# Eight instead of five feed-forward groups of a layer in seven-product form, three pairs of them adjacent; input sums on GpSimd; the kernel's beginning in another order

## The chip, the cores and the metric

The kernel runs on one core of a Trainium2 chip. Its engines are TensorE (PE; PEld is its weight load), VectorE (DVE), ScalarE (ACT), GpSimd (POOL) and SyncE (SP, which here only issues transfers). The metric is the device time of one execution in microseconds (us), the median of several runs.

## The reference

Two layers of a decoder trunk over 512 tokens of width 1024. Each layer mixes tokens by three parallel branches and then runs a gated feed-forward part with a causal convolution of three taps:

```python
D_MODEL = 1024; SEQ = 512; DEPTH = 2; D_FF = 3 * D_MODEL
for l in range(DEPTH):
    h = rms_norm(x, norm_mix[l])
    ...  # three branches, gated and merged
    x = x + merged @ w_out[l]
    h = rms_norm(x, norm_ffn[l])
    ff_g, ff_u = jnp.split(h @ ffn_up[l], 2, axis=-1)
    ff_g = causal_dwconv(ff_g, ffn_conv_w[l], ffn_conv_b[l])
    x = x + (jax.nn.gelu(ff_g) * ff_u) @ ffn_down[l]
return rms_norm(x, norm_final)
```

All is float32. The change concerns `h @ ffn_up[l]` and the first norm.

## The kernel before

**Precision by splitting.** Every float32 matrix is split into a rounded high part and the remaining low part; a product is three matmuls (low by high, high by low, high by high). `split_to` (line 149) does it for weights: ACT copies a 128x1024 block `raw` to `wh` (L169), DVE subtracts it to get `wl` (L170). `hl_split` does the same for activations (L182, L183). A block of 128x1024 weights is called a unit. The pool `wp` holds three pairs `wh`, `wl`, so the split of a unit waits until the matmuls of the third unit before it are done; its subtraction must end before the unit's own matmuls begin.

**The feed-forward part.** The normed activations lie transposed in `xh`, `xl` (128 rows x 8 blocks x 512 tokens). The 24 blocks of hidden channels come in three chunks of eight (HC = 8). A block needs a gate product and an up product, each one unit and 24 matmuls of 512 columns (`f_group`, L222 and L228); two blocks are a group of four units. After the products `hidden` runs the convolution (ACT L398, DVE L402 twice), the gelu (ACT L945), the product with the up half (DVE L950) and a split (L182, L183). After each chunk `t_section` (L265) multiplies by `ffn_down` and DVE adds the result to the residual (L918). This happens for two halves of the output.

**Seven-product form.** For the groups in `QUADS` the 2x2 block product (two halves of the contraction, gate and up as the other dimension; two halves of the tokens) is done with seven instead of eight block products. `x_sums` (line 930) makes sums of token halves once a layer with eight DVE instructions on 128x1024 (L934, L937) in the buffers S8 and S10 and splits the four that are multiplied into S1, S2, S3, S7. `quads` (line 953) then runs seven units of 24 matmuls of 256 columns (`q_mm`, L255). Its weights arrive as four blocks `quad`, two in S8 and two in S10, and are combined in place by four DVE additions (L168) before the splits. The seven weights have the letters a to g: a, f and d are blocks as they came (0, 2 and 3), b, c, e and g are sums. DVE also combines the seven results: L969, L970, L973, L979, L982. The products accumulate in PSUM banks t (a and d), s (b and f), s (c and g) and o (e).

**Order.** The tile framework makes an in-order list for each engine from the program and priorities; each engine then runs its list strictly in order and waits on semaphores. `plan` (line 113) is the order of the units' transfers and splits; in a group in `QUADS` it reads a b c d e, then the first unit of the next group, f g. `quads` runs that `f_group` between e and f. All weight transfers are on SP's queue, and the SP waits at the first one whose buffer is not free. S8 and S10 exist once, so the blocks of one seven-product group can be fetched only when the last splits that read the previous ones are done. `dma_to` and `split_to` run ahead of the use by two and three units.

**The beginning.** SP fetches the first block of x, the norm's gain row, weights and the remaining x; ACT and DVE norm a token block (`Norm.rows`), PE transposes its eight 128x128 blocks (`Norm.turn`, L350) and ACT and DVE split them. 18 matmuls on zeros (L110) stand ahead. `t_section` for the section `mv` starts as soon as the first token block is there; its first two units need only the contraction blocks 0 to 3.

## Time and profile before

| quantity | value |
|---|---|
| median of 3 runs (lowest, highest) | 1932.69 us (1932.33, 1933.23) |
| the profiled execution's own time | 1932.97 us |
| its span | 1931.2 us |
| PE busy | 1907.6 us (99%) |
| DVE busy | 1241.8 us (64%) |
| ACT busy | 825.3 us (43%) |
| POOL busy | 88.4 us (5%) |
| granted TensorE clock, mean | 0.996 |

The busy share of PE is the union of pipelined matmuls, so 99% says that hardly a moment passes without one in flight; how fast they follow each other is read from the starts in the timeline. The "chain that ended last" on the page follows the work back from the last instruction. A timeline row gives start, duration, engine, source line, operation, output and inputs, shape, number of merged instructions and, in brackets, idle time of the engine before it and what ended that. DVE's instructions overlap a little at their ends, so the step from one start to the next is shorter than a duration.

### The profile page before, as it was taken

How to read it: one execution, taken by the hardware profiler on the slowest of the kernel's cores; microseconds unless marked ns; L12 is line 12 of the kernel's file. 1: busy time of each engine (PE TensorE's matmuls, PEld its weight loads, DVE VectorE, ACT ScalarE, POOL GpSimd, SP SyncE). 2: the span in 40 equal slices, each digit the busy share in tenths (PEclk: the TensorE clock that was granted, in tenths of full speed). 3: DMA queues.
4: the chain of work that ended last, by engine and by line, in shares of the span. 5: the costliest groups of instructions: out<-in, count | busy, mean ns of one | idle time of the engine just before them, and what ended most of it. 6: DMA issues, size and time to landing. Idle time of an engine off the chain costs nothing.

```text
span 1931.2 us, 24656 instructions
## 1 busy us (share of the span) xinstructions
PE 1907.6 (99%) x9654; PEld 1591.0 (82%) x9654; DVE 1241.8 (64%) x2069; ACT 825.3 (43%) x1264; POOL 88.4 (5%) x154
## 2 busy tenths in 40 slices
PE   8999999999999999999999999999999999999997
PEld 6778888888788888888887888888877888888985
DVE  6897869644458557557558987794334765574763
ACT  5664444443335424334357444445323443352442
POOL 0012110000000000000000121000000000000000
PEclk9999999999999999999999999999999999999999
DMA  5248642322332323322332586223223243232222
GB/s 177 93 129 252 180 115 77 101 97 82 99 107 99 121 68 129 109 97 68 114 122 88 179 241 164 93 66 126 72 93 110 76 142 109 96 101 77 88 88 77
DMA packets 59349, 218.27 MB, mean 113 GB/s; under 512 B 7384, under 2 KB 7896, under 8 KB 57184
## 3 DMA queue, kind: packets, MB, share of 16 engines
q1 hardware_dynamic: 47088, 169.37, 26.9%
q0 software_dynamic: 10560, 43.54, 7.7%
q10 hardware_dynamic: 1584, 3.78, 0.6%
q8 instruction: 76, 1.25, 0.3%
q14 instruction: 41, 0.34, 0.1%
HBM read 196.72 MB, written 19.42 MB: 112 GB/s over the span
## 4 chain that ended last, share of the span: by engine, by line
PE 92%; DVE 3%; ACT 2%; issue 1%; DMA 1%; SPq 0%; POOLq 0%; ACTq 0%
PE A L222 34%; PE A L265 22%; PE A L228 17%; PE s L255 6%; PE t L255 3%; PE o L743 2%; PE o L255 1%; DVE wl L170 1%; PE o L669 1%; PE s L704 1%; PE t L756 1%; DVE m L402 1%; PE s L350 1%; ACT wh L169 1%; PE s L769 1%
## 5 line engine op out<-in xcount | busy, mean ns | idle before, releaser
L170 DVE TENSOR_TENSOR wl<-raw,wh 128x1024 fp32r<-128x1024 f32 x262 | 319.8, 1222 | 358.5 <-ACT wh L169 354.3
L222 PE MATMUL A<-xh,wl 128*128 128x512 f32 (+1 forms) x1392 | 545.5, 394 | 2.2 <-DVE m L402 0.7
L222 PE MATMUL A<-xl,wh 128*128 128x512 f32 (+1 forms) x1392 | 543.5, 392 | 0.0
L169 ACT ACTIVATE wh<-raw 128x1024 fp32r<-128x1024 f32 x262 | 276.6, 1057 | 334.0 <-PE A L265 141.7
L228 PE MATMUL A<-xh,wh 128*128 128x512 f32 (+1 forms) x1392 | 358.1, 393 | 0.0
L222 PEld LDWEIGHTS A<-xh,wl 128*128 128x128 f32 x1392 | 261.3, 188 | 63.4 <-DVE wl L170 3.5
L222 PEld LDWEIGHTS A<-xl,wh 128*128 128x128 f32 x1392 | 261.6, 188 | 59.5 <-issue 2.2
L228 PEld LDWEIGHTS A<-xh,wh 128*128 128x128 f32 x1392 | 255.5, 188 | 58.1 <-issue 1.2
L265 PE MATMUL A<-wh,S 128*128 128x512 f32 x832 | 261.8, 395 | 0.0
L265 PEld LDWEIGHTS A<-wh,S 128*128 128x128 f32 x832 | 155.9, 187 | 37.7
L265 PE MATMUL A<-wl,S 128*128 128x512 f32 x416 | 164.2, 395 | 0.0
L170 DVE TENSOR_TENSOR wl<-quad,wh 128x1024 fp32r<-128x1024 f32 x70 | 85.6, 1223 | 59.7 <-ACT wh L169 59.7
L169 ACT ACTIVATE wh<-quad 128x1024 fp32r<-128x1024 f32 x70 | 74.0, 1057 | 83.1 <-PE A L265 37.9
L402 DVE SCALAR_TENSOR_TENSOR m<-A,ch,m 128x511 f32<-128x511 f32 (+2 forms) x128 | 93.8, 743 | 10.1 <-ACT m L398 8.9
L265 PEld LDWEIGHTS A<-wl,S 128*128 128x128 f32 x416 | 78.0, 187 | 18.9
L255 PE MATMUL s<-S,wh 128*128 128x256 f32 x480 | 85.7, 281 | 0.0
L222 PE MATMUL A<-S,wl 128*128 128x512 f32 x192 | 75.9, 397 | 0.9 <-ACT S L594 0.9
L222 PE MATMUL A<-S,wh 128*128 128x512 f32 x192 | 75.2, 393 | 0.0
L255 PEld LDWEIGHTS s<-S,wh 128*128 128x128 f32 x480 | 74.0, 190 | 0.0
L846 ACT ACTIVATE th<-A 128x512 f32<-128x512 f32 x48 | 28.5, 595 | 104.7 <-PE A L228 78.1
L265 PE MATMUL A<-wx,S 128*128 128x512 f32 x288 | 69.3, 394 | 0.0
L758 ACT ACTIVATE g<-t 128x512 f32<-128x512 f32 (+2 forms) x48 | 25.1, 522 | 100.2 <-PE t L756 100.2
(264 smaller groups left out, 2802.6 us busy)
## 6 DMA issues: line engine op xcount, KB each, us to landing
raw<-in_wts_dram SPq DMA_DIRECT2D x274, 512.0 KB, 3.5
quad<-in_wts_dram SPq DMA_DIRECT2D x40, 512.0 KB, 4.4
S<-dh POOLq DMA_DIRECT2D x16, 512.0 KB, 6.9
S<-dl POOLq DMA_DIRECT2D x16, 512.0 KB, 7.8
dh<-th POOLq DMA_DIRECT2D x24, 256.0 KB, 4.3
dl<-m POOLq DMA_DIRECT2D x24, 256.0 KB, 3.6
S<-in_x_dram SPq DMA_DIRECT2D x4, 512.0 KB, 7.4
g<-gd POOLq DMA_DIRECT2D x8, 256.0 KB, 4.6
```

Of the source, the lines that this page charges most:

```text
L169: A.activation(out=h, in_=r, func=AF.Copy)
L170: V.tensor_tensor(out=l, in0=r, in1=h.bitcast(F32), op=ALU.subtract)
L222: T.matmul(ps, lhsT=a[:, k, :], rhs=b[:, k, :], start=(i == 0), stop=False)
L228: T.matmul(ps, lhsT=wh[:, k, :], rhs=b_h[:, k, :], start=False, stop=(i == n))
L255: T.matmul(ps[:, j * 256:(j + 1) * 256], lhsT=a[:, k, j * P:(j + 1) * P], rhs=x[b][:, k, :], start=start and j == 1 and i == 1, stop=j == ...
L265: T.matmul(ps, lhsT=a[k0 + j][:, tt], rhs=b[:, j, :], start=(start and i == 1), stop=(stop and i == n))
L350: ins = T.transpose(ps[:, c * P:(c + 1) * P], xn[:, k * P:(k + 1) * P], ident)
L402: V.scalar_tensor_tensor(out=acc[:, d:], in0=ps[:, :S - d], scalar=ch[:, cw + j * step:cw + j * step + 1], in1=acc[:, d:], op0=ALU.mult, o ...
L669: T.matmul(po[:, 0:129], lhsT=SD[:, sb * P:(sb + 1) * P], rhs=e.mv[:, sb, h, :], start=(sb == 0), stop=(sb == tb))
L743: T.matmul(po[:, h * 64:(h + 1) * 64], lhsT=pc[:, c * P:(c + 1) * P], rhs=e.av[:, c, h * 64:(h + 1) * 64], start=(c == 0), stop=(c == t))
L758: A.activation(out=pT[:, :n * P], in_=pp[:, :n * P], func=AF.Copy)
L846: A.activation(out=th, in_=pg, func=AF.Tanh, scale=0.5)
```

## The change

- `QUADS` has eight groups of a layer instead of five: (0,4), (0,6), (1,0), (1,2), (1,6), (2,0), (2,2), (2,6). Three pairs of a layer follow each other directly: (0,4) and (0,6), (1,0) and (1,2), (2,0) and (2,2).
- The order of the weights in such a group is a b c e d f g, with no unit of another group in between; `quads` runs a, b, c, e, d, then f and g, and no `f_group`.
- `x_sums` makes its eight sums on POOL.
- The beginning: the gain row comes on ACT's queue, the norm of the first layer is done by `squares` and `scaled`, the transposes of a token block are made in two halves, the instructions are tied in an order by `after`, and 24 instead of 18 matmuls on zeros stand ahead. Small transfers (`chan`, `rgw`, constants) come later.

```diff
@@ -37,7 +37,7 @@
 NK = 385
 
 
-QUADS = {(0, 4), (1, 0), (1, 4), (2, 0), (2, 4)}
+QUADS = {(0, 4), (0, 6), (1, 0), (1, 2), (1, 6), (2, 0), (2, 2), (2, 6)}
 SECTIONS = ("mv", "sm", "rx", "qk", "qi", "q", "k", "av", "mo")
 
 
...
@@ -106,7 +106,7 @@
     A.activation(out=warm, in_=half[:, 0:1], func=AF.Square)
     wz = S1("S9", (P, 512), BF)
     V.memset(wz, 0.0)
-    for _ in range(18):
+    for _ in range(24):
         T.matmul(accS(), lhsT=wz[:, 0:P], rhs=wz, start=True, stop=True)
 
     per = wts.shape[0] // depth
...
@@ -119,9 +119,8 @@
         for c in range(NH // HC):
             for g in range(HC // 2):
                 if (c, 2 * g) in QUADS:
-                    nxt = [(u + 4 + i, None) for i in range(4)]
-                    plan += [(u, o) for o in "abcde"] + nxt[:1] + [(u, o) for o in "fg"] + nxt[1:]
-                elif (c, 2 * g - 2) not in QUADS:
+                    plan += [(u, o) for o in "abcedfg"]
+                else:
                     plan += [(u + i, None) for i in range(4)]
                 u += 4
             plan += [(u + i, None) for i in range(HC)]
...
@@ -309,10 +310,37 @@
...
+        def squares(self, t):
+            lo, hi = slice(0, 512), slice(512, D)
+            with tc.high_priority():
+                xn = slot.tile([P, D], F32, tag=self.tags[t % len(self.tags)], name="xn")
+                ss = sml.tile([P, 2], F32, tag="ss", name="ss")
+                rs = sml.tile([P, 1], F32, tag="rs", name="rs")
+                if t < 2:
+                    V.tensor_tensor_reduce(out=xn[:, lo], in0=X(t, lo), in1=X(t, lo), scale=1.0, scalar=0.0,
+                                           op0=ALU.mult, op1=ALU.add, accum_out=ss[:, 0:1])
+                else:
+                    A.activation(out=xn[:, lo], in_=X(t, lo), func=AF.Square, accum_out=ss[:, 0:1])
+                A.activation(out=xn[:, hi], in_=X(t, hi), func=AF.Square, accum_out=ss[:, 1:2])
+                V.tensor_tensor(out=rs, in0=ss[:, 0:1], in1=ss[:, 1:2], op=ALU.add)
+                V.tensor_scalar(out=rs, in0=rs, scalar1=1.0 / D, scalar2=EPS, op0=ALU.mult, op1=ALU.add)
+                G.tensor_tensor(out=rs, in0=rs, in1=half[:, 0:1], op=ALU.pow)
+            self.xs[t], self.rs[t] = xn, rs
+
+        def scaled(self, t):
+            xn = self.xs.pop(t)
+            with tc.high_priority():
+                for cs in (slice(0, 512), slice(512, D)):
+                    v = V.scalar_tensor_tensor(out=xn[:, cs], in0=X(t, cs), scalar=self.rs[t], in1=self.g[:, cs],
+                                               op0=ALU.mult, op1=ALU.mult)
+            self.xn[t] = xn
+            return v
 
         def rows(self, t, sink=None):
             with tc.high_priority():
...
@@ -437,20 +461,45 @@
     for l in range(depth):
         if l == 0:
             res["src"] = x
+            nrm = Norm(norm_mix[0:1, :], ("S1", "S2", "S4", "S5"))
             nc.scalar.dma_start(out=ident, in_=const[:, K_ID:K_ID + P])
-            nrm = Norm(norm_mix[0:1, :], ("S1", "S2"), True)
-            nc.scalar.dma_start(out=kst[:, K_ID + P:], in_=const[:, K_ID + P:])
-            for t in range(1, NT):
-                dma_to(t)
+            dma_to(1)
+            nc.sync.dma_start(out=X(1), in_=x[P:2 * P, :])
+            dma_to(2)
+            for t in range(2, NT):
                 nc.sync.dma_start(out=X(t), in_=x[t * P:(t + 1) * P, :])
-            nrm.rows(0)
-            nrm.turn(0)()
-            split_to(1)
-            for t in range(1, NT):
-                nrm.rows(t)
-            mv_post = {t - 1: nrm.turn(t) for t in range(1, NT)}
-        ch = two.tile([P, NCH], F32, tag="ch", name="ch")
-        nc.scalar.dma_start(out=ch, in_=chan[l])
+            nrm.squares(0)
+            v = nrm.scaled(0)
+            with after(v):
+                split_to(1)
+            with after(st["pair"][0]), after(st["pair"][1]):
+                nrm.turn(0, (0,))()
+            with after(nrm.last[0]), after(nrm.last[1]):
+                nrm.squares(1)
+                split_to(2)
+            with after(st["pair"][0]), after(st["pair"][1]):
+                v = nrm.scaled(1)
+                ch0 = two.tile([P, NCH], F32, tag="ch", name="ch")
+                nc.scalar.dma_start(out=ch0, in_=chan[0])
+                nc.scalar.dma_start(out=kst[:, K_ID + P:], in_=const[:, K_ID + P:])
+                nrm.squares(2)
+                with after(v):
+                    nrm.turn(1, (0,))()
+                a1 = nrm.last
+                with after(a1[1]):
+                    v = nrm.scaled(2)
+                    nrm.turn(0, (1,))()
+                    nrm.turn(1, (1,))()
+                    nrm.squares(3)
+                    v = nrm.scaled(3)
+            mv_post = {0: nrm.turn(2), 1: nrm.turn(3)}
+        if l == 0:
+            ch = ch0
+        else:
+            ch = two.tile([P, NCH], F32, tag="ch", name="ch")
+            with after(a1[0]):
+                nc.scalar.dma_start(out=ch, in_=chan[l])
+        first = v
         e = SimpleNamespace()
         F_ = slice(96, 100)
         R_ = slice(64, 68)
...
@@ -931,10 +984,10 @@
             qa, qb = [S1(g, (P, 2, 4, 256)) for g in ("S8", "S10")]
             a = [qa[:, 0], qa[:, 1], qb[:, 0], qb[:, 1]]
             for n in (2, 3, 0, 1):
-                V.tensor_tensor(out=a[n], in0=xq[n][0].bitcast(F32), in1=xq[n][1].bitcast(F32), op=ALU.add)
+                G.tensor_tensor(out=a[n], in0=xq[n][0].bitcast(F32), in1=xq[n][1].bitcast(F32), op=ALU.add)
             for key, g, d, i0, i1, op in (("b", "S1", 3, 2, 3, ALU.subtract), ("c", "S2", 2, 0, 2, ALU.subtract),
                                           ("e", "S3", 0, 3, 0, ALU.subtract), ("f", "S7", 1, 1, 0, ALU.add)):
-                V.tensor_tensor(out=a[d], in0=a[i0], in1=a[i1], op=op)
+                G.tensor_tensor(out=a[d], in0=a[i0], in1=a[i1], op=op)
                 o = S1(g, (P, 2, 4, 256), dt=FR)
                 hl_split(a[d], o[:, 0], o[:, 1])
                 xq[key] = (o[:, 0], o[:, 1])
...
@@ -961,9 +1014,6 @@
                 A.activation(out=p1, in_=pa, func=AF.Copy)
             q_mm(pc, xq["b"])
             q_mm(pd, xq["c"])
-            q_mm(pa, xq[1], start=False)
-            with tc.high_priority():
-                A.activation(out=gt[:, :, 0:256], in_=three(pa), func=AF.Copy)
             q_mm(pb, xq["e"])
             with tc.high_priority():
                 V.tensor_tensor(out=u2, in0=p1, in1=pb, op=ALU.add)
...
@@ -971,7 +1021,9 @@
                 for j in range(2):
                     cs = slice(j * 256, (j + 1) * 256)
                     V.tensor_tensor(out=up[j][:, 256:512], in0=pc[:, cs], in1=tm[:, cs], op=ALU.subtract)
-            pg = f_group()
+            q_mm(pa, xq[1], start=False)
+            with tc.high_priority():
+                A.activation(out=gt[:, :, 0:256], in_=three(pa), func=AF.Copy)
             q_mm(pc, xq["f"], start=False)
             with tc.high_priority():
                 for j in range(2):
...
@@ -982,27 +1034,25 @@
                 V.tensor_tensor(out=gt[:, :, 256:512], in0=three(pd), in1=three(u2), op=ALU.add)
             for j in range(2):
                 hidden(i + j, m + j, gt[:, j, :], up[j])
-            return pg
 
         x_sums()
         nch = NH // HC
         for cidx in range(nch):
             hh = [S1("S4", dt=FR), S1("S6", dt=FR)]
...
```

The change moves instructions in the lists that the framework makes. Three places follow; between the beginning and the feed-forward part of a layer the lists of all engines are as before but for the names.

**DVE at the end of group (0,4) in the first layer, before.** L170 and L168 belong to the weights; `quad_5105` and `quad_5176` are this group's weights in S8 and S10, `raw` those of other groups; L402, L950 and L183 belong to `hidden`. From the split of g on:

```order
L170 TENSOR_TENSOR wl_5407<-quad_5105,wh_5406 128x1024
L973 TENSOR_TENSOR D_5252<-s_5245,g2_5251 128x256
L973 TENSOR_TENSOR D_5253<-s_5245,g2_5251 128x256
L170 TENSOR_TENSOR wl_5439<-raw_5376,wh_5438 128x1024
L979 TENSOR_TENSOR D_5252<-s_5245,g1_5250 128x256
L979 TENSOR_TENSOR D_5253<-s_5245,g1_5250 128x256
L170 TENSOR_TENSOR wl_5471<-raw_5411,wh_5470 128x1024
L982 TENSOR_TENSOR gate_5248<-s_5246,g1_5250 128x2x256
L170 TENSOR_TENSOR wl_5528<-raw_5442,wh_5527 128x1024
L402 SCALAR_TENSOR_TENSOR m1_5501<-gate_5248,ch_215,m1_5501 128x511
L402 SCALAR_TENSOR_TENSOR m1_5501<-gate_5248,ch_215,m1_5501 128x510
```

And now, with `quad_5113` the weights in S8 of (0,4), `quad_5353` and `quad_5418` those in S8 and S10 of (0,6); L181 is the split, L167 the addition of weights, L426 the convolution, L1034 the last gate half, L1031 the first up half. From the split of g of (0,4) to the split of b of (0,6):

```order
L181 TENSOR_TENSOR wl_5384<-quad_5113,wh_5383 128x1024
L1023 TENSOR_TENSOR D_5259<-s_5252,g2_5258 128x256
L1023 TENSOR_TENSOR D_5260<-s_5252,g2_5258 128x256
L1034 TENSOR_TENSOR gate_5255<-s_5253,g1_5257 128x2x256
L181 TENSOR_TENSOR wl_5415<-quad_5353,wh_5414 128x1024
L426 SCALAR_TENSOR_TENSOR m1_5476<-gate_5255,ch_197,m1_5476 128x511
L167 TENSOR_TENSOR quad_5353<-quad_5353 128x1024
L1031 TENSOR_TENSOR D_5259<-s_5252,g1_5257 128x256
L1031 TENSOR_TENSOR D_5260<-s_5252,g1_5257 128x256
L426 SCALAR_TENSOR_TENSOR m1_5476<-gate_5255,ch_197,m1_5476 128x510
L167 TENSOR_TENSOR quad_5353<-quad_5353,quad_5418 128x1024
L181 TENSOR_TENSOR wl_5447<-quad_5353,wh_5446 128x1024
```

Where the weights of the following units were split one after the other with the group's own results in between, the first two weights of the next seven-product group, their two additions, four result combinations and two steps of the convolution now stand in this order. The five other pairs stand alike.

**ACT at the start of the feed-forward part, before.** S1, S2, S3 and S7 are the high parts of the token sums (L182), `wh` those of weights; `raw_4919` is the sixth unit of the part:

```order
L182 ACTIVATE S1_4886<-S10_4880 128x1024
L398 ACTIVATE m1_5019<-A_4921,ch_215 128x512
L169 ACTIVATE wh_4915<-raw_4911 128x1024
L182 ACTIVATE S2_4890<-S10_4880 128x1024
L169 ACTIVATE wh_5029<-raw_4913 128x1024
L182 ACTIVATE S3_4894<-S8_4879 128x1024
L182 ACTIVATE S7_4898<-S8_4879 128x1024
L169 ACTIVATE wh_5066<-raw_4919 128x1024
```

And now (L180 for both; the sixth unit is `raw_4927`):

```order
L180 ACTIVATE wh_4923<-raw_4919 128x1024
L180 ACTIVATE wh_5037<-raw_4921 128x1024
L998 ACT_TABLE_LOAD
L998 ACTIVATE th_5031<-m1_5027 128x512
L180 ACTIVATE S1_4894<-S10_4888 128x1024
L422 ACTIVATE m1_5068<-A_5043,ch_197 128x512
L180 ACTIVATE S4_4909<-m1_5033 128x512
L180 ACTIVATE S2_4898<-S10_4888 128x1024
L180 ACTIVATE wh_5074<-raw_4927 128x1024
L180 ACTIVATE S3_4902<-S8_4887 128x1024
```

Two splits of weights and a gelu now stand ahead of the first sum's split, and the sixth unit's split stands behind the second sum's.

**DVE in the beginning, before.** L328, L330, L331 and L334 are the norm, L183 the split of transposed activations, L170 that of weights; from the second to the third unit of weights:

```order
L170 TENSOR_TENSOR wl_220<-raw_147,wh_219 128x1024
L328 TENSOR_TENSOR xn_193<-S12_97,grow_141 128x512
L183 TENSOR_TENSOR xl_91<-s_250,xh_90 128x4x128
L328 TENSOR_TENSOR xn_204<-S12_97,grow_141 128x512
L183 TENSOR_TENSOR xl_91<-s_257,xh_90 128x4x128
L330 TENSOR_TENSOR rs_195<-ss_194 128x1
L331 TENSOR_SCALAR rs_195<-rs_195 128x1
L330 TENSOR_TENSOR rs_206<-ss_205 128x1
L331 TENSOR_SCALAR rs_206<-rs_206 128x1
L334 SCALAR_TENSOR_TENSOR xn_193<-S12_97,rs_195,grow_141 128x512
L170 TENSOR_TENSOR wl_224<-raw_150,wh_223 128x1024
```

And now (L331, L332 and L340 the norm, L181 both splits), from the sums of squares of the third token block to the third unit of weights (`raw_243`):

```order
L331 TENSOR_TENSOR rs_202<-ss_201 128x1
L332 TENSOR_SCALAR rs_202<-rs_202 128x1
L340 SCALAR_TENSOR_TENSOR xn_183<-S11_96,rs_185,grow_152 128x512 x2
L181 TENSOR_TENSOR xl_91<-s_208,xh_90 128x4x128
L340 SCALAR_TENSOR_TENSOR xn_200<-S12_97,rs_202,grow_152 128x512 x2
L331 TENSOR_TENSOR rs_233<-ss_232 128x1
L181 TENSOR_TENSOR xl_91<-s_217,xh_90 128x4x128
L181 TENSOR_TENSOR xl_91<-s_224,xh_90 128x4x128
L332 TENSOR_SCALAR rs_233<-rs_233 128x1
L340 SCALAR_TENSOR_TENSOR xn_231<-S12_97,rs_233,grow_152 128x512 x2
L181 TENSOR_TENSOR wl_328<-raw_243,wh_327 128x1024
```

The third unit's split came ahead of the scaling of the last token block and now stands behind it; L328, the product with the gain ahead of the scaling, is gone.

## Rows read from the trace of the kernel before

**Rows 1.** The page: busy time of each engine; shares of the chain of work.

```profile
PE 1907.6 (99%) x9654; PEld 1591.0 (82%) x9654; DVE 1241.8 (64%) x2069; ACT 825.3 (43%) x1264; POOL 88.4 (5%) x154
...
PE 92%; DVE 3%; ACT 2%; issue 1%; DMA 1%; SPq 0%; POOLq 0%; ACTq 0%
```

**Rows 2.** Timeline of PE, where units begin, from group (1,0) on: start, duration, instruction.

```profile
708.02 0.28 PE L255 MATMUL t<-xh,wl 128*128 128x256 f32 x1
...
722.40 0.39 PE L222 MATMUL A<-xh,wl 128*128 128x512 f32 x1
...
727.99 0.28 PE L255 MATMUL s<-xh,wl 128*128 128x256 f32 x1
...
733.59 0.39 PE L222 MATMUL A<-xh,wl 128*128 128x512 f32 x1
...
750.39 0.28 PE L255 MATMUL t<-xh,wl 128*128 128x256 f32 x1
```

**Rows 3.** Timeline of DVE at the end of unit e and in the next group.

```profile
722.60 0.69 DVE L969 TENSOR_TENSOR g<-g,o 128x512 f32<-128x512 f32 x1
...
723.92 1.22 DVE L170 TENSOR_TENSOR wl<-quad,wh 128x1024 fp32r<-128x1024 f32 x1
725.06 0.75 DVE L973 TENSOR_TENSOR D<-s,g 128x256 f32<-128x256 f32 x2
...
742.39 0.69 DVE L950 TENSOR_TENSOR m<-th,D 128x512 f32<-128x512 f32 x1
743.00 1.22 DVE L168 TENSOR_TENSOR quad<-quad 128x1024 f32<-128x1024 f32 x1
744.13 0.75 DVE L402 SCALAR_TENSOR_TENSOR m<-A,ch,m 128x511 f32<-128x511 f32 x1
744.79 0.69 DVE L183 TENSOR_TENSOR S<-m,S 128x512 fp32r<-128x512 f32 x1
```

**Rows 4.** Timeline of DVE and SP at the split of g in (0,4).

```profile
636.76 1.22 DVE L170 TENSOR_TENSOR wl<-quad,wh 128x1024 fp32r<-128x1024 f32 x1
...
638.00 0.33 SPq L146 DMA_DIRECT2D quad<-in_wts_dram  x1
```

**Rows 5.** Instructions on the tiles `quad`: duration in ns (least, median, greatest); landing.

```profile
L169 ACT ACTIVATE wh<-quad x70: 1046/1060/1066, 609.8 to 1845.1; 128x1024 fp32r<-128x1024 f32 x70
...
DMA to landing us min/median/max: 3.4/4.4/6.7
```

**Rows 6.** Groups by line: busy us, mean ns of one, idle time ahead; POOL and DVE.

```profile
L332 POOL TENSOR_TENSOR rs<-rs,half 128x1 f32<-128x1 f32 x20 | 11.5, 573 | 776.1 <-DVE rs L331 750.1 <-ACT xh L182 19.6 <-ACT xn L327 6.5
L724 POOL TENSOR_TENSOR rp<-rs,half 128x4 f32<-128x4 f32 x8 | 9.6, 1199 | 42.2 <-DVE rs L722 42.2
...
L934 DVE TENSOR_TENSOR S<-xh,xl 128x1024 f32<-128x1024 f32 x8 | 9.4, 1220 | 0.1
```

**Rows 7.** Timeline at the feed-forward start: first token sum; sixth unit's first matmul.

```profile
578.05 1.23 DVE L934 TENSOR_TENSOR S<-xh,xl 128x1024 f32<-128x1024 f32 x1
...
604.04 0.40 PE L222 MATMUL A<-xh,wl 128*128 128x512 f32 x1
```

**Rows 8.** Timeline of PE in the beginning; the last row begins the section after `mv`.

```profile
8.69 0.33 PE L350 MATMUL s<-kst,xn 128*128 128x128 f32 x1 [2.09 <-ACT xn L333]
...
13.01 0.79 PE L265 MATMUL A<-wl,xh 128*128 128x512 f32 x1 [3.22 <-ACT xh L182]
...
22.41 0.33 PE L350 MATMUL s<-kst,xn 128*128 128x128 f32 x1 [0.16 <-ACT xn L333]
...
41.70 0.39 PE L222 MATMUL A<-xh,wl 128*128 128x512 f32 x1
```

**Rows 9.** Stretches: length, PE busy us (instructions), granted clock, DMA share, GB/s.

```profile
11.00:13.00 2.00, 0.00 (x0) 0.50 1.04 408
13.00:17.00 4.00, 4.00 (x11) 0.50 0.68 273
...
122.80:124.00 1.20, 0.49 (x3) 1.00 0.55 150
```

More of the change, by code (lines that the diff above doesn't have):

```diff
@@ L274, in t_units, with t_section @@
         return ws
-    def t_section(a_h, a_l, evac, hook=None, spare=()):
+    def t_section(a_h, a_l, evac, hook=None, spare=(), ahead=3, hold=()):
         ps = []
@@ L279, in t_section @@
         for half_ in range(2):
-            ws = t_units(4 * half_, 2, 3)
+            with ExitStack() as held:
+                for i in (hold if half_ else ()):
+                    held.enter_context(after(i))
+                ws = t_units(4 * half_, 2, 3 if half_ else ahead)
             for t in range(NT):
@@ L582, in sec_mo @@
             mn = sml.tile([P, 4], F32, tag="mn", name="mn")
-            V.tensor_scalar(out=mn, in0=ch[:, C_MN:C_MN + 4], scalar1=0.5, scalar2=None, op0=ALU.mult)
+            with after(first):
+                V.tensor_scalar(out=mn, in0=ch[:, C_MN:C_MN + 4], scalar1=0.5, scalar2=None, op0=ALU.mult)
             for c in range(4):
@@ L820, in sec_rx @@
             lam = ch[:, C_LAM:C_LAM + 4]
-            with after(nrm.last[0]):
+            with after(nrm.last[0]), after(first):
                 softplus(sp, lam)
@@ L824, in sec_rx @@
             e.sp8 = sml.tile([P, 2, 4], F32, tag="sp8", name="sp8")
-            V.tensor_scalar(out=e.sp8[:, 0, :], in0=lam, scalar1=-1.0, scalar2=0.0, op0=ALU.mult, op1=ALU.max)
+            with after(first):
+                V.tensor_scalar(out=e.sp8[:, 0, :], in0=lam, scalar1=-1.0, scalar2=0.0, op0=ALU.mult, op1=ALU.max)
             V.tensor_tensor(out=e.sp8[:, 0, :], in0=e.sp8[:, 0, :], in1=w_, op=ALU.add)
```

37 lines of the change are left out of this document (17 added, 20 removed).

## The prediction

> **What bounds the kernel now.** I read the page first: busy time of the engines and the shares of the chain. PE is busy 99% of the span and makes 92% of the chain [rows 1]. A high busy share alone doesn't say that PE works without gaps, since its matmuls overlap, so the next view is PE's timeline over the feed-forward part, at the starts of units [rows 2]: 708.02 to 722.40 is five seven-product units (a to e), so 2.876 us each; 722.40 to 727.99 one 512-column unit, 5.59; 727.99 to 733.59 units f and g together, 5.60; 733.59 to 750.39 three more 512-column units, 5.60 each. Each unit begins when the one before it is through. So what counts is PE's work and each wait that PE gets; work of DVE, ACT, POOL or SP counts only where PE comes to wait for it. In the beginning PE does wait: its first transposes start at 8.69, the first real matmul at 13.01 after 3.22 us of idling, and the section after `mv` at 41.70 [rows 8].
>
> Everything is summed against the profiled execution's own time, 1932.97 us, which is 0.28 above the median of the runs.
>
> **Six more groups in seven-product form.** Four units of 5.60 are 22.40 us. Seven units of 2.876 are 20.13. (Units f and g took 2.80 each, but just behind a unit of 512 columns, and now they stand behind d; with that figure it would be 19.98. I take 20.13, the row of the five others, and 19.98 as the other end.) Gain 2.27 each, 13.6 for six. The ten old groups lose the 512-column unit from their midst: with f and g at 2.876 they cost 0.15 more each, 1.5 in all, or nothing at the other end. Together **-12.1** (-14.5 to -12.1).
>
> **Waits inside a single group.** Unit g now follows d, so its split has from the end of e to the end of d, 2.88 us. Before, the split of g ended at 725.14, 2.74 after the end of e at 722.40 [rows 2, 3], behind two result combinations. 2.74 plus a tenth for the hand-over is just within 2.88; I count nothing, with 0.1 for each of 16 groups, 1.6, as the upper end.
>
> **The pairs.** This is the largest term. PE's list has the units in the order a b c e d g f, then a of the next group. Let 0 be the end of e. PE is through with f at 3 x 2.876 = 8.63 and wants a of the second group then, b at 11.5, c at 14.4.
> - *a.* Its block goes to S8, which is free when the split of g is done, at 2.74. SP issues at once (split ends 637.98, issue 638.00 [rows 4]). The `quad` transfers landed after 3.4 to 6.7 us, median 4.4 [rows 5]; the S10 pair, free since the split of f, is ahead by some 3 us, so I take 3.8: landed at 6.6. ACT's copy takes 1.06 [rows 5], so DVE's split runs from 7.7 to 8.95, and PE starts a at 9.05: a wait of 0.4.
> - *b.* On DVE's list seven instructions follow the start of that split up to the split of b: the convolution's first step, the addition for b, the two first up halves, the convolution's second step, the addition for c, and then the split of b. Steps from start to start: 1.13 for a 128x1024 instruction (743.00 to 744.13), 0.66 for a convolution step (744.13 to 744.79), 0.61 for 128x512 (742.39 to 743.00), and 0.66 for two half-width results, whose pair takes 0.75 [rows 3]. So 7.7 + 1.13 + 0.66 + 1.13 + 0.66 + 0.66 + 1.13 = 13.1, the split of b ends at 14.3, PE starts b at 14.4. It was through with a at 9.05 + 2.88 = 11.9: a wait of **2.5**.
> - *c.* Behind the split of b stand the product of `hidden`, a convolution step, the addition for e and the split of c: 13.1 + 1.13 + 0.61 + 0.66 + 1.13 = 16.6, done at 17.9. PE was through with b at 17.3: a wait of 0.65.
> - *e* and later: the split of e starts 1.13 + 0.66 + 0.61 after that of c, less than one unit of PE, so PE has caught up no more than DVE, and the waits end.
>
> Sum 3.5 a pair, six pairs: **+21**. It is DVE that is late: everything that the first group leaves behind (conv, halves, product) shares DVE with seven splits and four additions for the second, whereas before a unit of 512 columns stood in the middle and two or more groups of four behind. Faster transfers take away at most a's 0.4; with a landing of 5.8 instead of 3.8 it is 5.5. Ends: 3.0 and 5.5 a pair, 18 to 33. A gain is excluded, since PE can't start b ahead of its split.
>
> **After a pair or a single group** the next unit has 512 columns or belongs to `t_section`, 5.6 us each; SP's queue there holds the S10 and S8 blocks of a later group ahead of the third weight block, which is due 11.2 us after the first two. At 0.5 MB in 3.5 to 6.7 us that is covered; nothing.
>
> **Sums on POOL.** The trace has no such operation on POOL: its rows are 573 ns for 128x1 and 1199 for 128x4, a power; DVE does the sums in 1.22 us each [rows 6]. What they may cost follows from who waits. On ACT's list the second sum's split stands ahead of the sixth unit's split, which PE wants at 604.04 [rows 7]; ACT, DVE and the hand-over need 3.6 us for both, so the sixth POOL instruction must be done by 600.4. POOL can start at 578.05 like DVE [rows 7], so 22.3 us for six: up to 3.6 us each with the hand-overs, nothing is late. DVE's 1.22 is far below, a power on 1024 columns by the step from 1 to 4 columns (0.2 us a column) far above; addition is nearer to DVE's kind of row, and I take below 3.6: 0. The time DVE is relieved of, 8 x 1.2 us a layer, is no gain there, as PE waits for none of it.
>
> The Trainium skill, GPSIMD Engine Reference, "Performance versus the Vector engine", speaks against moving sums: a two-input addition of 2048 columns takes POOL 4497 ns, about twice DVE's time. As an estimate by that page one sum here is 2.25 us; six are 13.5, within the bound, and the sum would be the same. No run here shows it yet.
>
> **The beginning.** With 24 instead of 18 matmuls ahead PE stays busy to about 8, and the clock need not fall as it did, to half between 11 and 17 us [rows 9]. The first transposes are four, and the first real matmul can come near 10 instead of 13. But DVE sets the later pace: the third unit's split now stands behind the scaling of all token blocks, four of which cost two 0.66 steps each, and four residual subtractions, and by the lengths in the list it is done at about 22.2. From there 71 matmuls of 0.233 and eight transposes remain, 17.3 us: `mv` ends at 39.5 to 39.8. Before, PE had 72 and sixteen transposes to do from 22.41 and ended at 41.70 [rows 8]. So **-2.0**, and by a late landing or early one 0 to -3.
>
> **Sum.** 1932.97 - 12.1 + 21 - 2.0 = 1939.9, against the median 1939.6. Ends: 1932.7 - 14.5 + 18 - 3 = 1933 and 1932.7 - 12.1 + 1.6 + 33 + 0 = 1955.
>
> **The rivals.**
> 1. *Faster: the pairs don't wait.* If DVE gets the split of b done within a's 2.9 us, only the saved columns count: 1932.7 - 12.1 - 2.0 = **1918.6**. For it: DVE is busy only 64% over the whole kernel [rows 1]. Against it: that is an average, and the steps between the two splits add up to 5.4 us in the list's own order. It decides at 2.9.
> 2. *Half of it.* The transfers or the splits run further ahead than I read, and a pair costs 1.0 to 1.9: 1925 to 1932.
> 3. *Worse: the clock falls in the waits.* In the beginning PE stood idle from 9.8 and the granted clock was at 0.50, 1.2 GHz, from 11 to 17 us [rows 9]; behind a gap at 122.8 to 124.0, with PE busy 0.49 of 1.20, it stayed at 1.00. A wait of 2.5 lies between. If it falls and takes about as long to come back, some 6 us at half speed lose 3 each: 1939.6 + 18 = **1958**.
> 4. *Worse: POOL is slower than 3.6 us a sum*, alone or as DVE's splits use the same memory. At 4.5 the sixth unit waits 5 us in each of two layers: **1950**.
>
> **How the numbers follow.** Chances: my forecast 0.60 (1933 to 1946 mostly), rival 1 0.15, rival 2 0.10, rivals 3 and 4 together 0.15. A measurement of this kernel can tell about 0.2%, 3.9 us, from no change: faster is below 1928.8, slower above 1936.6. Faster: rival 1 and half of rival 2, 0.20. Same: the other half of rival 2 and the low end of my forecast, 0.15. Slower: 0.65. The range 1926 to 1952 leaves out rival 1 and a third of rivals 3 and 4. The likeliest case's own range is 1933 to 1946.
>
> **What would show it.** In PE's timeline of the changed kernel: 20.1 us from the start of a to the end of f in a group that stands alone, and 23 to 24 in the second group of a pair; a DVE-made idle of PE of about 2.5 ahead of b and 0.65 ahead of c, six times; PE's largest waits in the list of waits then name DVE `wl`, about 20 us in all. POOL busy about 20 us more a layer without PE waiting at the sixth unit. The section after `mv` at about 39.7. I am wrong if PE goes from a to b of a second group without a gap, if a wait moves to the transfers (ACT `wh` released by a transfer long after f), or if the granted clock is 0.50 anywhere behind the beginning.

## The result, and the profile after

The changed kernel takes 1943.89 us (median of four runs, 1943.66 to 1944.95), the kernel before 1932.64 on the same chip: a ratio of 1.0059, 95% interval 1.0041 to 1.0076. It is slower by 11.2 us; 6.9 were forecast, in a range of 1926 to 1952. The profiled execution has a span of 1941.8 us against 1931.2, 10.6 more, and the account below is made against these 10.6.

The page of the changed kernel, which answers to [rows 1]: busy time of each engine, and the shares of the chain of work.

```profile
PE 1899.1 (98%) x10092; PEld 1609.3 (83%) x10092; DVE 1300.7 (67%) x2139; ACT 845.8 (44%) x1288; POOL 131.3 (7%) x170
...
PE 84%; DVE 9%; issue 2%; ACT 2%; DMA 2%; POOL 0%; POOLq 0%; ACTq 0%; DVEq 0%
```

PE has 8.5 us less to do and the span is longer: DVE's share of the chain has gone from 3% to 9%. What PE waited for, from the list of waits of the changed kernel (us in total, times, longest):

```profile
PE s L253 <- DVE wl L181: 15.4, 10, 2.4
PE t L253 <- DVE wl L181: 2.2, 2, 1.5
PE s L253 <- DVE g L1020: 2.1, 6, 0.5
```

L253 is the 256-column unit of the seven-product groups; in the kernel before no row of the list names it. PE's timeline shows where these waits lie. The first group of the pair (0,4)-(0,6) starts at 620.94, the second at 641.22, the down section at 665.30; the last two rows are the start of a single group, (1,6), and the last matmuls of it (what follows starts at 796.08):

```profile
620.94 0.28 PE L253 MATMUL t<-xh,wl 128*128 128x256 f32 x1
...
641.22 0.39 PE L253 MATMUL t<-xh,wl 128*128 128x256 f32 x1
...
646.70 0.36 PE L253 MATMUL s<-S,wl 128*128 128x256 f32 x1 [2.34 <-DVE wl L181]
...
650.14 0.39 PE L253 MATMUL s<-S,wl 128*128 128x256 f32 x1 [0.34 <-DVE wl L181]
...
659.48 0.39 PE L253 MATMUL s<-xh,wl 128*128 128x256 f32 x1 [0.45 <-DVE g L1020]
...
665.30 0.40 PE L263 MATMUL A<-wl,S 128*128 128x512 f32 x1
...
775.96 0.28 PE L253 MATMUL t<-xh,wl 128*128 128x256 f32 x1
...
795.85 0.40 PE L253 MATMUL s<-S,wh 128*128 128x256 f32 x2
```

A single group takes 20.12 us (775.96 to 796.08), as forecast from [rows 2]. The pair takes 44.36 instead of 40.24: unit b of the second group starts 5.48 after unit a, which has 2.88 us of work, so it waits 2.60; c waits 0.66, g 0.61. (The figure in brackets is a little smaller, since a matmul's end is put later than the next one's start.) The six pairs are 4.1, 4.0, 4.7, 5.6, 4.9 and 4.7 us longer than two single groups: 28.0 in all, where 21 were forecast and 33 was the end of the range.

DVE's timeline over the first of these waits:

```profile
639.94 1.23 DVE L181 TENSOR_TENSOR wl<-quad,wh 128x1024 fp32r<-128x1024 f32 x1 [0.80 <-ACT wh L180]
641.08 0.74 DVE L426 SCALAR_TENSOR_TENSOR m<-gate,ch,m 128x511 f32<-128x511 f32 x1
641.74 1.22 DVE L167 TENSOR_TENSOR quad<-quad 128x1024 f32<-128x1024 f32 x1
642.88 0.75 DVE L1031 TENSOR_TENSOR D<-s,g 128x256 f32<-128x256 f32 x2
643.54 0.74 DVE L426 SCALAR_TENSOR_TENSOR m<-gate,ch,m 128x510 f32<-128x510 f32 x1
644.20 1.22 DVE L167 TENSOR_TENSOR quad<-quad 128x1024 f32<-128x1024 f32 x1
645.34 1.22 DVE L181 TENSOR_TENSOR wl<-quad,wh 128x1024 fp32r<-128x1024 f32 x1
```

From the start of the split of a (L181) to the start of that of b it is 645.34 - 639.94 = 5.40 us of DVE without a gap, the figure that the prediction had from its own steps. So the mechanism is there. But the total hides something that goes the other way. The changed kernel is faster in a place that the change doesn't touch, the down sections. Two rows three matmuls apart, of the kernel before and of the changed one:

```profile
669.52 0.39 PE L265 MATMUL A<-wl,S 128*128 128x512 f32 x1
...
670.22 0.39 PE L265 MATMUL A<-wl,S 128*128 128x512 f32 x1
```

```profile
671.45 0.39 PE L263 MATMUL A<-wl,S 128*128 128x512 f32 x1
...
672.13 0.39 PE L263 MATMUL A<-wl,S 128*128 128x512 f32 x1
```

Three matmuls take 0.70 us before and 0.68 after, 0.2333 and 0.2267 each over the first and the third quarter of the section, at a granted clock of 1.00 in both; in the second and fourth quarter it is 0.2333 and 0.2311. A down section of the first two chunks takes 43.98 instead of 44.80; with the last chunk's and the merge section that is 3.05 a layer, 6.1 us in all.

### The profile page after: what moved, and what is told of

Same layout as the page of the kernel before. It is cut to its first block, busy times and chain, and to the rows that moved or that the text cites. A ratio compares the mean times of both kernels' runs of the same rounds, so it can differ in the third digit from the quotient of the medians.

```text
span 1941.8 us, 25657 instructions
## 1 busy us (share of the span) xinstructions
PE 1899.1 (98%) x10092; PEld 1609.3 (83%) x10092; DVE 1300.7 (67%) x2139; ACT 845.8 (44%) x1288; POOL 131.3 (7%) x170
## 4 chain that ended last, share of the span: by engine, by line
PE 84%; DVE 9%; issue 2%; ACT 2%; DMA 2%; POOL 0%; POOLq 0%; ACTq 0%; DVEq 0%
PE A L220 29%; PE A L263 22%; PE A L226 15%; PE s L253 6%; DVE wl L181 3%; PE t L253 2%; PE o L793 2%; PE o L253 2%; DVE m L426 2%; DMA quad<-in_wts_dram 1%; ACT wh L180 1%; PE o L719 1%; PE s L754 1%; PE t L806 1%; DVE quad L167 1%
## 5 line engine op out<-in xcount | busy, mean ns | idle before, releaser
L181 DVE TENSOR_TENSOR wl<-raw,wh 128x1024 fp32r<-128x1024 f32 x238 | 295.0, 1241 | 294.5 <-ACT wh L180 292.4
L220 PE MATMUL A<-xh,wl 128*128 128x512 f32 (+1 forms) x1200 | 470.3, 394 | 3.1 <-DVE m L426 1.6
L220 PE MATMUL A<-xl,wh 128*128 128x512 f32 (+1 forms) x1200 | 467.7, 392 | 0.0
L180 ACT ACTIVATE wh<-raw 128x1024 fp32r<-128x1024 f32 x238 | 250.9, 1056 | 223.6 <-PE A L263 101.7
L226 PE MATMUL A<-xh,wh 128*128 128x512 f32 (+1 forms) x1200 | 309.4, 392 | 0.0
L180 ACT ACTIVATE wh<-quad 128x1024 fp32r<-128x1024 f32 x112 | 118.2, 1057 | 161.7 <-PE A L263 37.6
L181 DVE TENSOR_TENSOR wl<-quad,wh 128x1024 fp32r<-128x1024 f32 x112 | 136.8, 1223 | 56.3 <-ACT wh L180 55.7
L253 PE MATMUL s<-S,wh 128*128 128x256 f32 x768 | 141.5, 285 | 0.0
L253 PE MATMUL s<-S,wl 128*128 128x256 f32 x384 | 110.6, 288 | 15.4 <-DVE wl L181 15.4
L253 PEld LDWEIGHTS s<-S,wh 128*128 128x128 f32 x768 | 121.2, 194 | 0.0
L426 DVE SCALAR_TENSOR_TENSOR m<-A,ch,m 128x511 f32<-128x511 f32 (+2 forms) x104 | 75.9, 742 | 21.1 <-ACT m L422 20.1
L253 PEld LDWEIGHTS s<-S,wl 128*128 128x128 f32 x384 | 74.5, 194 | 17.3 <-issue 15.1
L167 DVE TENSOR_TENSOR quad<-quad 128x1024 f32<-128x1024 f32 x64 | 78.2, 1222 | 1.0
```

Of the source, the lines that this page charges most:

```text
L167: V.tensor_tensor(out=r, in0=r, in1=add, op=ALU.add)
L180: a = A.activation(out=h, in_=ps, func=AF.Copy)
L181: v = V.tensor_tensor(out=l, in0=ps, in1=h.bitcast(F32), op=ALU.subtract)
L220: T.matmul(ps, lhsT=a[:, k, :], rhs=b[:, k, :], start=(i == 0), stop=False)
L226: T.matmul(ps, lhsT=wh[:, k, :], rhs=b_h[:, k, :], start=False, stop=(i == n))
L253: T.matmul(ps[:, j * 256:(j + 1) * 256], lhsT=a[:, k, j * P:(j + 1) * P], rhs=x[b][:, k, :], start=start and j == 1 and i == 1, stop=j == ...
```

## The experiments

All times are medians, and the kernel before was run beside each (1932.6 to 1933.0).

**Five groups, none behind another.** `QUADS` of the kernel before in the changed kernel:

```diff
-QUADS = {(0, 4), (0, 6), (1, 0), (1, 2), (1, 6), (2, 0), (2, 2), (2, 6)}
+QUADS = {(0, 4), (1, 0), (1, 4), (2, 0), (2, 4)}
```

> The changed kernel with the five groups a layer that had the form before, none behind another; all else as changed. It costs three groups a layer of 22.4 instead of 20.1 us, 13.7 us in all. Theory (the waits of 28 us in the changed trace belong to the pairs alone, 4.0 to 5.6 us at each of six): 1943.9 + 13.7 - 28 = 1929.6, and no wait of PE on DVE wl above 0.2 us in the feed-forward part. Rival (the waits come from the unit order a b c e d g f or from the sums, and stay at single groups): 1943.9 + 13.7 = 1957.6, or between.

1928.16 us, ratio 0.9977 (0.9967 to 0.9987). The list of waits has no row of L253 any more. 15.7 us less than the changed kernel: 28.0 less waiting, 13.7 more for three groups a layer in four products, and 1.4 left over, of which 0.8 is PE's wait at L426 (1.6 in the changed kernel, 0.8 here). So the waits belong to the pairs, neither to the order of the units nor to the sums.

**The second group's additions left out.**

```diff
-                if add is not None:
+                if add is not None and u not in second:
```

`second` holds the first unit of every group that stands right behind another in seven-product form.

> The changed kernel without the four additions of weights (b, c, e, g) of the second group of each pair: these units work on single blocks, so the sums of products of these groups are left out of what is computed; everything else runs, transfers, splits and products among it. Theory (DVE's list is what is late): the split of b starts 2 x 1.13 us earlier in DVE's list, that of c 3 x 1.13: b waits 0.3 to 0.4 instead of 2.60 us, c and g nothing, a as before; 28 - 22.5 us of waits are left, 1920 to 1923. Rival (the blocks of the second group land late, or ACT's copies are): PE waits as before, 1942 to 1945.

1919.66 us, ratio 0.9933 (0.9913 to 0.9953), 24.2 less than the changed kernel. PE at the first pair, units a and b of the second group:

```profile
640.78 0.39 PE L255 MATMUL t<-xh,wl 128*128 128x256 f32 x1
...
643.75 0.28 PE L255 MATMUL s<-S,wl 128*128 128x256 f32 x1
```

2.97 instead of 5.48: b waits 0.1. The transfers and ACT's copies are the same as before, so it was DVE's list. Of 28 us some 3 are left: 0.1 ahead of b at each pair, the rest ahead of a, where the second group's first block comes from memory, 1.36 of them at one pair.

**The same additions on POOL.**

```diff
-                    V.tensor_tensor(out=r, in0=r, in1=add, op=ALU.add)
+                    (G if u in second else V).tensor_tensor(out=r, in0=r, in1=add, op=ALU.add)
```

> The changed kernel with the four additions that the second group of a pair makes on its weights moved from DVE to POOL; nothing else. Theory (DVE is late: its steps between the splits set the start of b and c): two additions of 1.13 us go out of the way of b's and c's split each, while POOL needs 2.4 to 3.3 us for one, so b's wait falls from 2.6 to about 0.2 to 1.4 and c's from 0.66 to 0.3 or less; 2 to 3.5 us a pair, six pairs: 1923 to 1932. Rival 1 (the transfers of the second group land late): no change, 1943 to 1945. Rival 2 (an addition on POOL is 3.3 us or longer beside DVE, and POOL becomes the one that is waited for): 1940 to 1955.

1964.12 us, ratio 1.0161 (1.0146 to 1.0177): 20 us slower than the changed kernel, beyond both rivals. The wait of b is 4.57 and that of c 2.4, part of the latter at a lower clock: behind b's wait the granted clock falls to 0.50 at all six pairs. DVE and POOL at the first pair:

```profile
640.49 0.75 DVE L428 SCALAR_TENSOR_TENSOR m<-gate,ch,m 128x511 f32<-128x511 f32 x1
641.15 0.75 DVE L1033 TENSOR_TENSOR D<-s,g 128x256 f32<-128x256 f32 x2
641.82 2.22 DVE L428 SCALAR_TENSOR_TENSOR m<-gate,ch,m 128x510 f32<-128x510 f32 x1
644.79 2.00 DVE L1005 TENSOR_TENSOR m<-th,D 128x512 f32<-128x512 f32 x1 [0.76 <-ACT th L1000]
646.72 1.21 DVE L183 TENSOR_TENSOR wl<-quad,wh 128x1024 fp32r<-128x1024 f32 x1
```

```profile
640.71 5.54 POOL L169 TENSOR_TENSOR quad<-quad 128x1024 f32<-128x1024 f32 x2 [41.06 <-DVE wl L183]
```

Two additions run on POOL from 640.71 to 646.25, 2.8 us each. DVE's step of 0.74 us takes 2.22, the product of 0.69 takes 2.00, and both end at about the time when an addition of POOL ends (643.5 and 646.25). The steps of L1033 in the same stretch, with one input in PSUM, take their usual 0.75 for two. So DVE doesn't run slower beside POOL; an instruction with two inputs in SBUF stands until POOL's is through. The Trainium skill, SBUF — State Buffer, "Who interferes with whom", states just that: a DVE instruction with two SBUF inputs contends with a GpSimd instruction that reads SBUF, and the one that comes second blocks. The trace agrees (2.22 against 0.74 us). The experiment is no test of the transfers, as it was meant to be: it replaced DVE's 1.13 us by a stand of 1.3 to 2.2.

**The sums back on DVE.**

```diff
-                G.tensor_tensor(out=a[n], in0=xq[n][0].bitcast(F32), in1=xq[n][1].bitcast(F32), op=ALU.add)
+                V.tensor_tensor(out=a[n], in0=xq[n][0].bitcast(F32), in1=xq[n][1].bitcast(F32), op=ALU.add)
```

(and the four sums of sums alike)

> The changed kernel with the eight sums of activations a layer back on DVE. Theory (PE waits for neither engine there, so it doesn't matter who makes them): 1943.9, within 0.8. Rival 1 (POOL's 2.4 to 3.3 us a sum hold DVE up beside it and cost PE time): 1938 to 1942. Rival 2 (DVE, now relieved by 10 us a layer, had been late there): 1946 to 1950.

1943.42 us, ratio 1.0053 (1.0036 to 1.0069): the same as the changed kernel within about 1 us, and no better than that, since in the profiled executions the clock falls behind b's wait at four pairs here and at two in the changed kernel (see the pairs below). On POOL the sums take 2.38 to 3.28 us each in the changed kernel, within the 3.6 of the prediction. The estimate of 2.25 that the prediction made by the Trainium skill, GPSIMD Engine Reference, "Performance versus the Vector engine", is below all of them. POOL does hold DVE up there: the splits of the sums, from the groups by line of the changed kernel and of this one (busy us, mean ns):

```profile
L181 DVE TENSOR_TENSOR S<-S,S 128x1024 fp32r<-128x1024 f32 x8 | 13.0, 1621 | 0.0
```

```profile
L181 DVE TENSOR_TENSOR S<-S,S 128x1024 fp32r<-128x1024 f32 x8 | 9.6, 1218 | 0.0
```

1.62 instead of 1.22 us, in a stretch where PE waits for neither.

**The beginning alone.** The kernel before with the changed kernel's `squares`, `scaled`, halves of transposes, 24 zero matmuls and order of transfers; its groups and sums as before.

> The kernel before with the new beginning alone (six sums and all feed-forward groups as before). The buffers S4 and S5 then lie as in the changed kernel, which was worth 6.1 us by itself. Theory (the new beginning costs 0.9 us: the section after mv starts 0.1 later, and PE waits for DVE at about 120 us 0.9 longer): 1926.8 + 0.9 = 1927.7. Rival (the beginning gains the 2.0 us that were forecast and the loss came from elsewhere): 1924.8.

1926.69 us, ratio 0.9971 (0.9960 to 0.9982). Since this kernel has its buffers where the changed one has them, it is to be held against the kernel with the old beginning and only these buffers moved (the next experiment), 1926.83: 0.1 us less, or 0.2 more by what each gains on the kernel before beside it (5.9 and 6.1), so nothing that these runs can tell. The new beginning neither gains 2.0 nor costs 0.9. The 0.9 is a wait at about 124 us that differs between kernels with the same beginning: 1.60 in the changed kernel, 0.81 with five groups, 0.34 here. Its rows in the changed kernel and here:

```profile
124.98 0.50 PE L220 MATMUL A<-xh,wl 128*128 128x512 f32 x1 [1.60 <-DVE m L426]
```

```profile
123.49 0.50 PE L221 MATMUL A<-xh,wl 128*128 128x512 f32 x1 [0.34 <-DVE m L427]
```

**Where the tiles lie: the buffers.** The kernel before, with S4 and S5 allocated ahead of S3, as in the changed kernel, where the norm of the beginning uses them first. S3 is 64 bytes longer than the other buffers, so whatever lies behind it is shifted by 64.

```diff
+            for g in ("S1", "S2", "S4", "S5"):
+                G.memset(S1(g)[:, 0, 0:8], 0.0)
```

> The kernel before, with two of its buffers (S4, S5) laid ahead of S3 in SBUF, where the changed kernel has them: four small writes to the buffers ahead of everything set that; nothing else is changed. Theory (the 0.2267 instead of 0.2333 us from matmul to matmul in the down and merge sections of the changed kernel comes from where the tiles lie, 145696 and 153888 instead of 170336 and 178528): 6.1 us less, 1926 to 1927.5, with 0.2267 us a matmul in the down sections behind the first chunk. Rival (it comes from the work ahead of these sections: 256-column units, or no 512-column unit in between): 1932.6, and 0.2333.

1926.83 us, ratio 0.9969 (0.9957 to 0.9981), 6.1 less, as the theory had it. The down section:

```profile
672.04 0.39 PE L265 MATMUL A<-wl,S 128*128 128x512 f32 x1
...
672.72 0.40 PE L265 MATMUL A<-wl,S 128*128 128x512 f32 x1
```

0.68 for three, and the section takes 43.99 us. So the changed kernel's gain in these sections is a side effect of the order in which its new beginning first uses its buffers.

**Where the tiles lie: the activations.** Three kernels move `xh` and `xl`, the moving tiles of all feed-forward units of 512 columns, by 32, by 160 and (modulo 512) by 416 bytes: smaller tiles that lay behind them are allocated ahead of them. The weight tiles, the stationary ones, stay. For 160 bytes:

```diff
+    half = one.tile([P, 4], F32, name="half")
+    nc.gpsimd.memset(one.tile([P, NT, 8], F32, tag="wT", name="wT"), 0.0)
     xh = one.tile([P, KD, S], FR, name="xh")
```

> The kernel before, with one 32-byte tile allocated ahead of the activations xh and xl, so that these lie 32 bytes further on, at 32 bytes past a multiple of 128 like the weight tiles; every other tile that PE reads stays where it was. Theory (PE's step depends on how the addresses of the moving and the stationary tile stand to each other modulo 128 bytes): the 512-column units with xh as the moving tile go from 0.2335 to about 0.227 us a matmul; some 3400 of them, -20 to -24 us: 1909 to 1913. Rival (it depends on something else in the placement, or not on xh): 1932.6.

> The kernel before with the activations xh and xl 160 bytes further on in SBUF, so that their place is the same modulo 512 bytes as that of the weight tiles; every other tile that PE reads stays. Theory (PE's step from matmul to matmul is 0.2267 us where the moving and the stationary tile stand alike modulo 512, as in the down sections of the changed kernel, and 0.232 to 0.2335 where they don't): the 512-column units with xh moving go to 0.2267, 3438 matmuls x 0.0067 = -23 us: 1909 to 1913. Rival (the place modulo 512 isn't what counts): between 1926 and 1933.

> The kernel before with xh and xl 416 bytes further on, modulo 512 (256 bytes beside the weight tiles modulo 512, alike modulo 256); every other tile that PE reads stays. Theory (512 bytes is what counts): PE's step with xh moving is between 0.230 and 0.2335 us, 1925 to 1933. Rival (256 bytes is enough): 0.2267 us as with 160 bytes, 1914 to 1916.

By 32 bytes: 1927.97 us, ratio 0.9975 (0.9966 to 0.9985). By 160: 1914.98, ratio 0.9909 (0.9894 to 0.9924). By 416: 1914.68, ratio 0.9913 (0.9895 to 0.9931). The same stretch of a 512-column unit in the kernel before, by 32, by 160 and by 416 bytes:

```profile
739.66 0.39 PE L222 MATMUL A<-xh,wl 128*128 128x512 f32 x1
...
741.06 0.39 PE L222 MATMUL A<-xh,wl 128*128 128x512 f32 x1
```

```profile
733.76 0.40 PE L222 MATMUL A<-xh,wl 128*128 128x512 f32 x1
...
735.14 0.86 PE L228 MATMUL A<-xh,wh 128*128 128x512 f32 x3
```

```profile
733.86 0.39 PE L223 MATMUL A<-xh,wl 128*128 128x512 f32 x1
...
735.22 0.61 PE L229 MATMUL A<-xh,wh 128*128 128x512 f32 x2
```

```profile
733.80 0.39 PE L224 MATMUL A<-xh,wl 128*128 128x512 f32 x1
...
735.16 0.61 PE L230 MATMUL A<-xh,wh 128*128 128x512 f32 x2
```

Six matmuls take 1.40, 1.38, 1.36 and 1.36 us; in the first three kernels the step over three groups of 24 is 0.2333, 0.2322 and 0.2267. Modulo 512, `xh` lies 352 bytes beside the weight tiles in the kernel before, 384 with 32 bytes, 0 with 160 and 256 with 416. Alike modulo 128 isn't enough (32 bytes), alike modulo 256 is (416 bytes, 512 not needed). The weight tiles stay where they are in all these kernels, so no run tells a place of the two tiles against each other from a place that each of them must have by itself. Nor does the place alone set the step where the tiles are not alike: the down section takes 44.59 instead of 44.80 us in each of these three kernels, though none of the tiles that it reads was moved. The 160 bytes bring 17.6 of the 23 us that were expected: with PE faster, a wait for DVE at about 120 us is 2.6 instead of 0.7, and one for a transfer takes up to 2.6.

**All of it together.** S3 behind all other buffers and the 160 bytes, so that every moving and stationary tile of the 512-column units stands alike modulo 256; the kernel before, the changed one, and the changed one with six groups a layer, none behind another.

> The kernel before with every tile that PE reads in its 512-column units at the same place modulo 512 bytes: xh and xl 160 bytes further on, and the buffer S3 (64 bytes longer than the others) behind S4, S5, S10, S7 and S6. Theory (the place modulo 512 sets PE's step): on top of the kernel with xh and xl moved (1915.0) the down and merge sections go from 0.2322 to 0.2267 us, 1248 matmuls, 5.5 to 7 us: 1908 to 1910, with 0.2267 in all sections. Rival (the two placements don't add, or DVE's work becomes what PE waits for): 1912 to 1915.

> The changed kernel with the same placement. Theory (the pairs' waits and the placement are separate things): a normal group then takes 21.8 us instead of 22.4, so six more groups in seven-product form gain 1.65 each, 9.9; the ten others lose 1.4; the waits of the pairs stay at 27 to 29, as the units with waits are all of 256 columns: 16 to 20 us above the kernel before in this placement, 1924 to 1930. Rival (part of the 28 us came from where the tiles lie, for instance from DVE's and PE's reads together): less than 12 above it.

> The changed kernel in the same placement with six groups a layer in seven-product form, none behind another: the second and fourth of the first chunk, the first and third of the others. Theory (single groups don't wait): the kernel before in this placement, less two more groups at 1.65, plus 1.4 for the order of the units: 1906 to 1908, the fastest of all. Rival (the sums for the first such group, now one group earlier, come late; or the group behind which the down section follows at once delays it): 1910 to 1916.

The kernel before in this placement: 1904.42 us, ratio 0.9854 (0.9838 to 0.9871), the fastest of all, 28.6 us under the kernel before, 39.5 under the changed one, and 4 below what was expected, for which no reason was found. The changed kernel in it: 1923.43, ratio 0.9951 (0.9936 to 0.9966). That is 19.0 more at equal placement; at the placement of S4 and S5 alone it was 1943.89 - 1926.83 = 17.1. The wait of b at the first pair is what it was:

```profile
639.90 0.36 PE L254 MATMUL s<-S,wl 128*128 128x256 f32 x1 [2.35 <-DVE wl L182]
```

Six single groups: 1929.91, ratio 0.9984 (0.9974 to 0.9993), a miss of 22 us. The first such group, now one earlier, needs S8 and S10 for its blocks, and the sums are still in them: POOL works on these until 591.78, and SP issues the first block at 592.99.

```profile
601.89 0.58 PE L254 MATMUL t<-xh,wl 128*128 128x256 f32 x1 [11.36 <-DVE wl L182]
```

11.4 us in one layer and 11.1 in the other. So sums on POOL cost nothing only where the first such group comes late enough; whether sums on DVE, which are shorter, would have been in time here, no run shows. Behind that wait the clock was lower; stretches of this kernel, with length, busy us of PE, PEld, DVE, ACT and POOL, granted clock, DMA share and GB/s:

```profile
601.90:605.50 3.60, 3.60 (x17) 3.60 (x18) 3.56 (x3) 2.11 (x2) 0.00 (x0) 0.50 0.00 0
607.00:612.00 5.00, 5.00 (x44) 5.00 (x44) 3.78 (x4) 2.72 (x3) 0.00 (x0) 1.00 0.00 0
```

## Why the prediction was right, and where it was not

In the account of the profiled executions the changed kernel is 10.6 us longer; the terms, as forecast and as measured:

| term | forecast | measured |
|---|---|---|
| six more groups | -13.6 | -13.7 (20.12 against 22.40) |
| ten old groups, f and g not behind 512 columns | +1.5 | +1.4 |
| waits inside single groups | 0 (up to 1.6) | 0 |
| pairs | +21 (18 to 33) | +28.0 |
| sums on POOL | 0 | 0 (1943.4 against 1943.9) |
| beginning | -2.0 (-3 to 0) | +0.9 in this execution, nothing clear by the experiment |
| place of the tiles | none | -6.1 |
| sum | +6.9 | +10.5 |

**The pairs** were right in mechanism, place and engine, and 7 us short in size. By steps: a waits 3.0 in all where 2.4 were forecast, from 0.1 to 1.6 by what the first block's transfer takes, which was the step's uncertainty. b waits 2.60 at every pair (2.5 forecast). c and e were forecast at 3.9 for six and take 5.8: 0.66 at four pairs, as forecast, and 1.56 at the third and the sixth, where the granted clock falls to 0.50 behind the wait of b (rows under the rivals) and PE works at half speed for some 3 us. DVE's list is the same at the third pair as at the second, so the 0.9 more at each of the two is the clock's. g was forecast at nothing and takes 3.1. The step that failed there reads "the waits end": I followed the splits alone. Unit g, which PE runs ahead of f, adds into the accumulator of c, and must wait until DVE has read it (L1020); in the second group of a pair this read stands behind the split of g itself on DVE, in the first group ahead of it:

```profile
657.01 0.68 DVE L1019 TENSOR_TENSOR g<-g,o 128x512 f32<-128x512 f32 x1
657.61 1.22 DVE L181 TENSOR_TENSOR wl<-quad,wh 128x1024 fp32r<-128x1024 f32 x1
658.75 0.68 DVE L1020 TENSOR_TENSOR g<-g,s 128x512 f32<-128x512 f32 x1
```

PE is through with d at 658.87 and starts g at 659.48. The rest, 0.5, is small gaps behind the pairs.

**The beginning** failed by its steps behind the zero matmuls. These did what was forecast: the clock stays at 1.00 where [rows 9] had 0.50, and the first real matmul starts at 10.71 instead of 13.01 [rows 8]. But the third unit's split lets PE start at 23.32, not 22.2, and I had PE run through from there, which it doesn't:

```profile
23.32 0.50 PE L263 MATMUL A<-wl,xh 128*128 128x512 f32 x1 [1.09 <-DVE wl L181]
...
36.10 0.50 PE L263 MATMUL A<-wl,xh 128*128 128x512 f32 x1 [0.65 <-DVE wl L181]
...
41.83 0.39 PE L220 MATMUL A<-xh,wl 128*128 128x512 f32 x1
```

The fourth unit's split is late as well, and `mv` ends at 41.83 against 41.70. A faster start moved the wait to the next split on the same engine, whose work had not become less.

**The place of the tiles** was in no step: durations of [rows 2] were taken over to units that the change doesn't touch. That term hid the errors of the two others: without it the forecast of 6.9 stands against 16.6, still inside the range of 1926 to 1952 (1949.3) but outside the likeliest case's own range of 1933 to 1946.

**The rivals.** That the pairs don't wait, or half, is refuted by the six waits of 2.60. The third rival came true in part: the clock fell behind two of them. Stretches of the changed kernel, with length, busy us of PE, PEld, DVE, ACT and POOL, granted clock, DMA share and GB/s: the wait of b at the first pair, the same wait at the third, and the time behind the latter:

```profile
644.10:646.70 2.60, 0.26 (x4) 0.08 (x2) 2.60 (x4) 2.33 (x5) 0.00 (x0) 1.00 0.00 0
863.30:865.90 2.60, 0.28 (x3) 0.08 (x2) 2.60 (x4) 2.32 (x5) 0.00 (x0) 1.00 0.00 0
867.50:870.50 3.00, 3.00 (x16) 3.00 (x16) 3.00 (x5) 1.49 (x2) 0.00 (x0) 0.50 0.00 0
```

PE had done next to nothing in both waits, and the clock fell behind the one and not behind the other. It fell at the third and the sixth pair of this execution, at four pairs in the traces of the kernel with the sums on DVE and of the changed kernel with all tiles alike, and at all six with the additions on POOL; what decides it stays open. So a sign that the prediction named for being wrong, a granted clock of 0.50 behind the beginning, did appear. It costs little: without the wait of a, these two pairs take 4.5 and 4.6 us more than two single groups, the four others 4.0. The rival counted 3 us each; but while b runs at half speed the split of c gets done, so c no longer waits, and g waits 0.34 instead of 0.61. POOL stayed under 3.6 us a sum.

## What to carry to other kernels

An engine that is busy two thirds of the time on average can still be the bound in a stretch: before two pieces of the same kind of work are put side by side, count what each engine has to do per piece against the time that the bounding engine gives, the leftovers of the first piece and the reads that free an accumulator among it. A change of what is used first moves tiles, and with them the time of sections that it doesn't touch, so compare such sections first and make the account at equal placement. Read the granted clock behind every wait of a kind, not behind the first alone. Moving an elementwise step from DVE to POOL isn't free for DVE where both read SBUF.

## What the runs showed of the hardware

- PE's step of a 512-column matmul depends on where its two tiles lie: 0.2267 us where the moving and the stationary one are alike modulo 256 bytes, 0.2311 to 0.2333 where some or all are 64, 96 or 128 bytes apart by that measure, at the same granted clock. Putting all of them alike took 28.6 us off the kernel before, with no instruction of its work changed. The 256-column units kept 0.1200 in all placements. The Trainium skill, TensorE: Matmul & The Clock Gate, "Step-by-step: what each phase is for", holds that loading the next weights takes no SBUF bandwidth from the running matmul, by which the place of the two wouldn't matter; the measurement decides, and it does. Whether it is these two reads that collide, no run here shows; the steps repeat in patterns of three and seven matmuls, which I can't explain.
- A DVE instruction with two SBUF inputs stands until POOL's running addition ends (2.22 instead of 0.74 us); one with an input in PSUM doesn't (0.75 for two, as ever).
- A wait of 2.60 us, in which PE worked 0.26 to 0.28 us, was followed by a granted clock of 0.50 for some 3 us at two of six pairs of one execution, and by 1.00 at the four others.
- The wait for DVE at about 120 us is 0.3 to 1.7 us in kernels with the same beginning, and 2.6 where the tiles are moved; its cause stays open.
